# Branch gates computed in a stage of their own by Strassen's algorithm, through DRAM scratch

## The chip, the cores and the metric

The kernel runs on one core of a Trainium2 chip. The metric is the device time of one execution in microseconds; of several runs the median is taken. PE is the matrix engine, DVE the vector engine, ACT the scalar engine, POOL the GpSimd engine; SP only issues DMAs. Each engine works through its own queue in order.

## The reference

One step of a diffusion backbone with one layer, 1024 features, 1024 latent tokens and 256 context tokens. Cut to what matters here:

```python
mod = (silu(cond) @ w_ada + b_ada)[:, None, :]
sh1, sc1, gt1, sh2, sc2, gt2 = split(mod, 6)
u = rmsnorm(x, g_norm1) * (1 + sc1) + sh1
xp, su, sv, q, k, v, o_pre, gate_pre, br_pre = split(u @ w_in, points)
y_a, y_b, y_c = pool_branch(xp), sgu_branch(su, sv), mlstm_branch(q, k, v, o_pre, gate_pre)
branches = einsum('btrc,rcd->btrd', stack([y_a, y_b, y_c]), w_branch)
gates = sigmoid(br_pre).reshape(B, T, 3, 1024)
x = x + gt1 * (sum_r(gates * branches) @ w_out)
u2 = rmsnorm(x, g_norm2) * (1 + sc2) + sh2
x = x + gt2 * (relu(u2 @ w_ff1) ** 2 @ w_ff2)
```

`cond` differs between latent and context tokens, so each part of `mod` has two rows. All inputs and results are float32.

## The kernel before

Features lie on the 128 partitions and tokens along the free axis, in three groups of columns: 512 and 512 latent tokens and 256 context tokens (`GROUPS`). Every float32 product is made of three products of a reduced type: an operand is split into `hi` (a cast) and `lo` (the rest), and hi*hi, hi*lo and lo*hi are summed in PSUM. ACT makes the cast of a weight (L94) and DVE the rest (L95). A projection of 1024 features to a tile of 128 therefore takes 8 x 3 matmuls per group of columns (`dense`, L118 to L126). PSUM has eight banks: three of the tag `mm`, for projections, and five of the tag `sd`.

The stages follow one another: norms and adaLN; the mLSTM heads; the SGU's v projection; the pooling branch; the SGU branch, which for each of four tiles mixes (L707, evicted by DVE at L711), projects u (`p_su`, evicted by DVE at L719) and splits the product into hi and lo (L115, L116); the branch stage; the output projection and the second norm; FF1; FF2. A scheduler reorders instructions of neighbouring stages within each engine's queue, so stages overlap a little.

**The branch stage** (L734 to L769) goes over the SGU branch, the pooling branch and the mLSTM branch, and in each over eight feature tiles `d` and three groups: gate product (`br`, 24 matmuls), sigmoid on ACT (L754), branch product (`pb`, 12 matmuls, L756 to L761), and on DVE the product of the two (L766, or L768 and the sum at L769) into the merged sum in `z`. The SGU's result stays in SBUF; the other two are read back from DRAM (`scr_ya`, `scr_yc`). Weights are loaded as 512 KB tiles of two `raw` buffers.

**The adaLN pieces** (`mod_piece`, L424 to L448) are the part of `mod` that is needed only after the branches. After half of the units of the branch stage one piece is made: a 512 KB load of `w_ada`, four multiply-adds on DVE (L437, L439) into two accumulators. Each fourth piece ends a group: POOL reduces both accumulators over the partitions (L446), adds the bias `bt` (L444, L447) and writes the row to `scr_mod` (L448). There are eight groups.

**FF1** (`Pair`, L942 to L1018) is computed by a Strassen algorithm of Winograd's form already: two feature tiles and two halves of the latent tokens make a 2 x 2 block product of 7 products instead of 8, each of 4 x 3 matmuls on 512 columns. The left sides are the weight blocks and four sums of them (L1002, on DVE); the right sides are the quarters `B11` to `B22` of the activations and four sums of those, `T1` to `T4`, each split into hi and lo. The context tokens are multiplied in the ordinary way, 48 matmuls of 256 columns a pair. DVE and ACT add the products out of PSUM into `z`. During FF1, POOL makes sums of FF2's weights (L1048).

## Time and profile before

| | before |
|---|---|
| median of three runs | 2010.93 us (2009.26 to 2013.67) |
| profiled execution | 2009.92 us |
| its span, first to last instruction | 2008.1 us |
| mean granted clock | 0.994 |
| PE, DVE, ACT, POOL busy | 97%, 59%, 39%, 19% |
| branch stage, DVE and POOL busy from 700 to 750 us | 18.20 and 11.07 of 50 us |

A row of the timeline is a start, a duration, an engine, a line, an operation, its output and inputs, and a count; in brackets stands the idle time of the engine ahead of it and what ended it. A row of the waits names who waited for whom: total, times, longest. Rows that group instructions by line end with busy time, mean ns of one, and the idle time ahead of them. Matmuls overlap in the array, so the distance between two starts, not the duration shown, is what one of them costs. Line numbers are those of the kernel the row comes from; order rows of the kernel after the change have its own lines.

### The profile page before, as it was taken

To read this page: it belongs to the slowest core of one execution; us is meant where nothing else is said; L and a number is where in the kernel's file an instruction comes from. 1 tells how busy PE (TensorE), PEld (TensorE's weight loads), DVE (VectorE), ACT (ScalarE), POOL (GpSimd) and SP (SyncE) were. 2 spreads that over 40 slices of the span, in tenths; PEclk is the share of its full clock that TensorE was granted. 3 is DMA by queue.
4 is the path that set the end of the run, shared out by engine and by line. 5 is a ranking of instruction groups with operands and counts; after the bars stand their busy time and mean duration, and the time that the engine had idled before them with its cause. 6 is when DMAs were issued, how large, how long until landed. Compare 5 with 4: busy or idle time off the path is not lost. (4 is left out here: it accounts for less than half of the span.)

```text
span 2008.1 us, 28473 instructions
## 1 busy us (share of the span) xinstructions
PE 1948.0 (97%) x10688; PEld 1677.5 (84%) x10688; DVE 1182.4 (59%) x1997; ACT 793.0 (39%) x1620; POOL 375.3 (19%) x372
## 2 busy tenths in 40 slices
PE   6999999998999999999999998999999999999997
PEld 3788888996888888888889997888888878888886
DVE  6684443448753235445526678887776665654675
ACT  6634454653211111111114465444445545443443
POOL 2000001108211122222201004444431120000002
PEclk9999999999999999999999999999999999999999
DMA  8011111113321252244215444677774496655544
GB/s 327 22 35 48 51 45 42 60 46 102 140 65 62 64 188 75 74 130 143 84 32 200 168 135 175 245 252 250 252 274 137 155 357 218 191 177 157 155 136 154
DMA packets 122683, 282.30 MB, mean 141 GB/s; under 512 B 14256, under 2 KB 28464, under 8 KB 120496
## 3 DMA queue, kind: packets, MB, share of 16 engines
q1 hardware_dynamic: 85456, 199.12, 30.8%
q0 software_dynamic: 14240, 53.56, 7.0%
q10 hardware_dynamic: 22848, 27.80, 3.9%
q8 instruction: 84, 1.38, 0.3%
q14 instruction: 55, 0.45, 0.1%
HBM read 204.36 MB, written 76.06 MB: 140 GB/s over the span
## 5 line engine op out<-in xcount | busy, mean ns | idle before, releaser
L754 ACT ACTIVATE sg<-br 128x512 f32<-128x512 f32 (+1 forms) x72 | 37.9, 526 | 305.3 <-PE br L126 290.4
L1048 POOL TENSOR_TENSOR z<-z 128x512 f32<-128x512 f32 x64 | 96.9, 1515 | 119.6 <-DMA z<-in_w_ff 109.9
L446 POOL PARTITION_ALL_REDUCE acc<-acc x16 | 54.2, 3430 | 325.8 <-DVE acc L439 325.8
L439 DVE SCALAR_TENSOR_TENSOR acc<-wb,scond,acc 128x512 f32<-128x512 f32 x112 | 82.3, 791 | 17.1 <-DMA wb<-in_w_ada 16.9
L768 DVE TENSOR_TENSOR sg<-pb,sg 128x512 f32<-128x512 f32 (+1 forms) x48 | 28.7, 599 | 101.8 <-PE pb L761 96.8
L1153 POOL TENSOR_TENSOR rs_y<-rs_y,neghalf 128x1 f32<-128x1 f32 x10 | 9.1, 912 | 333.9 <-DVE rs_y L1152 333.8
L766 DVE TENSOR_TENSOR z<-pb,sg 128x512 f32<-128x512 f32 (+1 forms) x24 | 14.4, 600 | 79.6 <-PE pb L761 79.6
L960 ACT ACTIVATE z<-z 128x512 f32<-128x512 f32 x64 | 40.6, 634 | 47.2 <-DVE z L1011 34.9
L95 DVE TENSOR_TENSOR lo_br<-raw_br,hi_br 128x1024 fp32r<-128x1024 f32 x24 | 37.5, 1564 | 28.1 <-ACT hi_br L94 27.9
L94 ACT CAST hi_br<-raw_br 128x1024 fp32r<-128x1024 f32 x24 | 25.2, 1050 | 70.2 <-DMA raw_br<-in_w_in 40.7
L131 POOL TENSOR_TENSOR rs_h<-rs_h,neghalf 128x4 f32<-128x4 f32 (+1 forms) x12 | 11.9, 992 | 207.9 <-DVE rs_h L130 207.8
L1002 DVE TENSOR_TENSOR z<-z 128x512 f32<-128x512 f32 x64 | 45.6, 716 | 0.6
L1039 POOL DMA_DIRECT2D scr_s<-x x48 | 26.5, 552 | 92.9 <-DVE x L1033 85.2
L583 DVE SCALAR_TENSOR_TENSOR yc<-th,ccol,z 128x512 f32<-128x512 f32 (+1 forms) x12 | 7.9, 660 | 57.3 <-PE th L581 57.3
L961 ACT ACTIVATE z<-z 128x512 f32<-128x512 f32 x64 | 40.4, 631 | 1.5
L94 ACT CAST hi_wb<-raw_wb 128x1024 fp32r<-128x1024 f32 x12 | 12.6, 1047 | 63.8 <-PE br L125 44.0
L95 DVE TENSOR_TENSOR lo_wo<-raw_wo,hi_wo 128x1024 fp32r<-128x1024 f32 x24 | 29.2, 1220 | 14.1 <-ACT hi_wo L94 14.1
L865 ACT ACTIVATE po<-z 128x256 f32<-128x256 f32 x40 | 15.5, 387 | 52.4 <-DVE z L864 45.8
L666 POOL TENSOR_TENSOR z<-z 128x1024 f32<-128x1024 f32 (+13 forms) x20 | 35.4, 1781 | 3.0 <-ACT z L651 3.0
L769 DVE TENSOR_TENSOR z<-z,sg 128x512 f32<-128x512 f32 (+1 forms) x48 | 34.7, 724 | 1.2
L862 DVE TENSOR_TENSOR po<-po,gt 128x256 f32<-128x256 f32 x40 | 17.1, 428 | 26.4 <-PE po L860 23.2
L447 POOL TENSOR_TENSOR acc<-acc,bt 1x512 f32<-1x512 f32 x16 | 20.7, 1309 | 58.3 <-issue 58.3
(3368 smaller groups left out, 7293.3 us busy)
## 6 DMA issues: line engine op xcount, KB each, us to landing
z<-in_w_ff SPq DMA_DIRECT2D x64, 512.0 KB, 5.2
wb<-in_w_ada SPq DMA_DIRECT2D x32, 512.0 KB, 3.7
scr_t<-z POOLq DMA_DIRECT2D x16, 1024.0 KB, 5.2
raw_br<-in_w_in SPq DMA_DIRECT2D x24, 512.0 KB, 3.4
raw_wo<-in_w_out SPq DMA_DIRECT2D x24, 512.0 KB, 4.2
scr_h<-z ACTq DMA_DIRECT2D x48, 256.0 KB, 4.4
scr_s<-x POOLq DMA_DIRECT2D x48, 256.0 KB, 3.1
wa<-in_w_ada SPq DMA_DIRECT2D x32, 256.0 KB, 5.2
```

What stands on the lines that cost most here:

```text
L94: A.copy(hi, raw)
L95: eng.tensor_tensor(lo, raw, hi.bitcast(F32), ALU.subtract)
L439: V.scalar_tensor_tensor(acc[j], wa[:, k2, :], scond[:, k, j : j + 1], acc[j], ALU.mult, ALU.add)
L446: G.partition_all_reduce(acc[j], acc[j], P, bass.bass_isa.ReduceOp.add)
L666: eng.tensor_tensor(at(dst, a, b), at(src, a - l, b - l), at(src, a + r_, b + r_), ALU.add)
L754: A.activation(sg[:, :n], ps[:, :n], AF.Sigmoid)
L768: V.tensor_tensor(sg[:, :n], pb[:, :n], sg[:, :n], ALU.mult)
L769: V.tensor_tensor(mg(d, g), mg(d, g), sg[:, :n], ALU.add)
L960: A.activation(t, t, AF.Relu)
L961: A.activation(t, t, AF.Square)
L1002: V.tensor_tensor(out, x, y, op)
L1048: G.tensor_tensor(out, x, y, ALU.subtract)
```

## The change

1. **A gate stage.** After the SGU, the 24 gate tiles are computed as 12 pairs by the FF1 algorithm (`GatePair`, a subclass of `Pair`): 84 matmuls of 512 columns and 48 of 256 per pair. The four weight sums are on POOL (`eng` is `G`; for FF1 it stays DVE). ACT applies the sigmoid, and ACT's queue stores the gates to `scr_g`, five halves of a tile a pair of features.
2. **Right sides.** `quarter_sums` rebuilds the 16 raw quarters of `u` as hi + lo and subtracts them into the four sums, 32 DVE operations, written behind the SGU's first tile. `split_sum` splits T4, T3, T2 and T1 around the first two pairs.
3. **The branch stage** has branch products alone. All three branches, the SGU's too (`scr_yb`), and the gates are read from DRAM into slots on SP's queue.
4. **adaLN pieces** are 64 of 256 KB instead of 32 of 512 KB, all in the gate stage: after pair n, up to piece 6n. Their raws lie in `z`.
5. **Pools.** The pools of weight and temporary tiles are closed ahead of the gates. One pool (`q1`: four tiles `e`, six `th`, six `w`, where it had five, six `s`) serves gates, branches, output projection and FF1; weights are loaded in halves of 512 columns (`load_half`). `slot` has 59 buffers, where it had 60. FF2 takes every second raw tile from `s`.

The diff, cut to its core:

```diff
-    sp = pa.enter_context(tc.tile_pool(name="sp", bufs=60))
+    sp = pa.enter_context(tc.tile_pool(name="sp", bufs=59))
...
-    def mod_piece(i):
-        b, kk = i // 4, i % 4
...
+    def mod_piece(i, raw):
+        b, k = i // 8, i % 8
...
+        SP.dma_start(raw, w_ada[k * P : (k + 1) * P, 2048 + b * 512 : 2048 + (b + 1) * 512])
+        for j in range(2):
+            if k == 0:
+                V.tensor_scalar(acc[j], raw, scond[:, k, j : j + 1], None, ALU.mult)
+            else:
+                V.scalar_tensor_tensor(acc[j], raw, scond[:, k, j : j + 1], acc[j], ALU.mult, ALU.add)
+        if k < 7:
             return
...
+    def quarter_sums(raw):
+        for kk in range(4):
+            b11, b21, b12, b22 = raw["B11"][kk], raw["B21"][kk], raw["B12"][kk], raw["B22"][kk]
+            if raw is u_raw:
+                for t, k, g in ((b11, kk, 0), (b12, kk, 1), (b22, kk + 4, 1), (b21, kk + 4, 0)):
+                    hi, lo = uT[k][g]
+                    V.tensor_tensor(t, hi.bitcast(F32), lo.bitcast(F32), ALU.add)
+            for out, x, y in ((b11, b12, b11), (b12, b22, b12), (b22, b22, b11), (b21, b22, b21)):
+                V.tensor_tensor(out, x, y, ALU.subtract)
...
         proj(I_SU + ci, f"su{ci}", ev_su)
-        ys.append(parts)
+        if ci == 0:
+            quarter_sums(u_raw)
...
+                self.eng.tensor_tensor(out, x, y, op)
+            ps = self.prod(self.w22, "T4")
+            A.copy(self.b2, ps)
+            ps = self.prod(split(a11, f"s2_{self.name}"), "T2")
...
+    for n in range(NGP):
+        if n not in gates:
+            gate_pair(n)
+            gates[n].begin()
+            gates[n].contexts()
+        gates[n].rest()
+        gates[n].store(ORDER[n // 4], n % 4 * 2)
+        del gates[n]
+        while n > 0 and piece < 64 and piece < 6 * n:
+            mod_piece(piece, zs(12 + piece % 4))
+            piece += 1
...
-            w = load_w(w_in[I_BR + r * KT + d], f"br{r}_{d}")
...
-                ps = ps_mm(f"br{r}_{d}_{g}")
-                dense(ps, w, uT, g)
-                sg = tmp(f"sg{r}_{d}_{g}")
-                A.activation(sg[:, :n], ps[:, :n], AF.Sigmoid)
+                sg = slot(f"sg{r}_{d}_{g}", F32)
+                SP.dma_start(sg[:, :n], scr_g[r][d][:, t0 : t0 + n])
```

The order of instructions on DVE in the SGU stage. Before, between the last evictions of the pooling branch (`ya`) and those of the first SGU tile (`mt`, with `p_su` its projection in PSUM):

```order
566 L690 SCALAR_TENSOR_TENSOR ya_0_1_4909<-pp_0_4906,ccol,ya_0_0_4908 128x512
567 L690 SCALAR_TENSOR_TENSOR ya_1_1_4918<-pp_1_4915,ccol,ya_1_0_4917 128x512
568 L690 SCALAR_TENSOR_TENSOR ya_2_1_4927<-pp_2_4924,ccol,ya_2_0_4926 128x256
569 L711 SCALAR_TENSOR_TENSOR mt_0_4939<-mx_0_4934,ccol,z 128x512
570 L711 SCALAR_TENSOR_TENSOR mt_1_4946<-mx_1_4941,ccol,z 128x512
571 L719 TENSOR_TENSOR mt_0_4939<-mt_0_4939,p_su_4959 128x512
```

After, the same place on DVE, where L704 and L706 are the quarter sums and L686, L737 and L744 stand for L690, L711 and L719:

```order
589 L704 TENSOR_TENSOR z<-u2h_421,u2l_422 128x512
590 L686 SCALAR_TENSOR_TENSOR ya_1_1_4919<-pp_1_4916,ccol,ya_1_0_4918 128x512
591 L706 TENSOR_TENSOR z<-z 128x512
592 L686 SCALAR_TENSOR_TENSOR ya_2_1_4928<-pp_2_4925,ccol,ya_2_0_4927 128x256
593 L706 TENSOR_TENSOR z<-z 128x512 x2
594 L737 SCALAR_TENSOR_TENSOR mt_0_4940<-mx_0_4935,ccol,z 128x512
595 L737 SCALAR_TENSOR_TENSOR mt_1_4947<-mx_1_4942,ccol,z 128x512
596 L706 TENSOR_TENSOR z<-z 128x512
597 L737 SCALAR_TENSOR_TENSOR mt_2_4952<-mx_2_4949,ccol,z 128x256
598 L737 SCALAR_TENSOR_TENSOR mt_0_5092<-mx_0_5087,ccol,z 128x512
599 L706 TENSOR_TENSOR z<-z 128x512
600 L744 TENSOR_TENSOR mt_0_4940<-mt_0_4940,p_su_4960 128x512
```

Up to DVE's row 552 both orders agree; from there to row 600 the order after has 28 of the 32 new operations ahead of the first multiplication by `p_su`.

The order on POOL, where an all-reduce is an `ISA` row with its accumulator, and an `ISA` row without one stands ahead of a change to another kind of instruction. Before, in the branch stage, one group of adaLN pieces:

```order
102 L446 ISA
103 L446 ISA acc_0_5442<-acc_0_5442 128x512
104 L446 ISA acc_1_5443<-acc_1_5443 128x512
105 L444 DMA bt_5597<-in_b_ada 1x16x32
106 L447 ISA
107 L447 TENSOR_TENSOR acc_0_5442<-acc_0_5442,bt_5597 1x512
108 L447 TENSOR_TENSOR acc_1_5443<-acc_1_5443,bt_5597 1x512
109 L448 DMA scr_mod<-acc_0_5442 16x1x32
110 L448 DMA scr_mod<-acc_1_5443 16x1x32
```

After, in the gate stage, the second group's all-reduce and the sums of gate pair 3 (L848), with the next group's all-reduce behind them:

```order
114 L442 ISA acc_0_6181<-acc_0_6181 128x512
115 L442 ISA acc_1_6182<-acc_1_6182 128x512
116 L848 ISA
117 L848 TENSOR_TENSOR z<-z 128x512 x3
118 L440 DMA bt_6408<-in_b_ada 1x16x32
119 L848 TENSOR_TENSOR z<-z 128x512
120 L443 TENSOR_TENSOR acc_0_6181<-acc_0_6181,bt_6408 1x512
121 L443 TENSOR_TENSOR acc_1_6182<-acc_1_6182,bt_6408 1x512
122 L444 DMA scr_mod<-acc_0_6181 16x1x32
123 L444 DMA scr_mod<-acc_1_6182 16x1x32
124 L442 ISA
125 L442 ISA acc_0_6416<-acc_0_6416 128x512
```

Weight sums, on which PE's product T2 depends, now stand in one queue with the all-reduces, in turns.

## The prediction

> **What bounds the kernel now.** I read the page first, then busy time in windows over the stages that change, then PE's waits there, then the timeline of PE, DVE and POOL where work is added.

> The page, share of each engine; below it stretches of 50 us (PE, weight loads, DVE, ACT, POOL; granted clock, DMA share, GB/s), and what PE waited for from 450 to 1200 us:

> ```profile
> PE 1948.0 (97%) x10688; PEld 1677.5 (84%) x10688; DVE 1182.4 (59%) x1997; ACT 793.0 (39%) x1620; POOL 375.3 (19%) x372
> ```
> ```profile
> 500.00:550.00 50.00, 47.76 (x248) 39.19 (x249) 37.46 (x52) 12.87 (x19) 12.82 (x17) 0.93 0.37 130
> 550.00:600.00 50.00, 50.00 (x272) 43.44 (x270) 25.78 (x43) 5.89 (x7) 2.83 (x1) 1.00 0.23 70
> 700.00:750.00 50.00, 50.00 (x263) 43.12 (x262) 18.20 (x24) 8.14 (x12) 11.07 (x7) 1.00 0.60 190
> ...
> 1200.00:1250.00 50.00, 44.66 (x239) 36.59 (x238) 44.70 (x79) 31.90 (x66) 19.17 (x12) 1.00 0.44 160
> 1300.00:1350.00 50.00, 50.00 (x268) 43.25 (x266) 39.54 (x54) 23.66 (x44) 22.98 (x24) 1.00 0.74 258
> ```
> ```profile
> PE pp L686 <- DVE xp L684: 5.4, 1, 5.4
> PE pp L686 <- issue: 3.1, 1, 3.1
> PE fB L938 <- ACT a_0h L929: 1.2, 1, 1.2
> PE po L860 <- DVE lo_wo L95: 0.5, 1, 0.5
> ```

> The branch stage (549 to 1042 us) is pure PE: 50.00 of 50 us, full clock, no wait of PE after 502 us, DVE at a third. Fewer matmuls there are time won one for one, as long as the new stage feeds PE as well. FF1 (1300 us), the model of the new gate stage, also reaches 50.00, with DVE at 39.5 of 50 and POOL at 23.

> **Part 1, matmuls removed.** One of the profile's modelled matmul durations (0.39) is no price; the distance between starts is. Twelve steps of 512 columns (517.34 to 520.06) and 23 of 256 (526.76 to 529.50):

> ```profile
> 517.34 0.39 PE L126 MATMUL p_su<-u0h,lo_su 128*128 128x512 f32 x1
> 520.06 0.39 PE L126 MATMUL p_su<-u4h,lo_su 128*128 128x512 f32 x1
> ...
> 526.76 0.28 PE L124 MATMUL p_su<-u0c,hi_su 128*128 128x256 f32 x1
> 529.50 0.28 PE L126 MATMUL p_su<-u7c,lo_su 128*128 128x256 f32 x1
> ```

> That is 0.227 and 0.119 us each. Before, two gate tiles cost 96 + 48 matmuls, 27.5 us; after, 84 + 48, 24.8 us. Twelve pairs save 144 x 0.227 = **32.7 us**. The branch products keep their count (24 tiles x (24 x 0.227 + 12 x 0.119) = 165 us).

> **Part 2, quarter sums in the SGU stage.** DVE gets 16 additions hi + lo (L704) and 16 subtractions (L706) of 128x512, in its queue ahead of the evictions that PE waits for. The order keeps DVE's rows up to the end of this L673, at 507.4:

> ```profile
> 505.77 1.63 DVE L673 TENSOR_TENSOR z<-z 128x1024 f32<-128x1024 f32 x1
> 507.43 1.10 DVE L684 TENSOR_TENSOR xp<-z,xp 128x512 f32<-128x512 f32 x1
> 508.46 0.74 DVE L690 SCALAR_TENSOR_TENSOR ya<-pp,ccol,ya 128x512 fp32r<-128x512 f32 x1
> 509.12 1.72 DVE L684 TENSOR_TENSOR xp<-z,xp 128x512 f32<-128x512 f32 x1
> ...
> 512.01 1.23 DVE L666 TENSOR_TENSOR z<-z 128x1024 f32<-128x1024 f32 x1
> 513.15 1.22 DVE L95 TENSOR_TENSOR lo_su<-raw_su,hi_su 128x1024 fp32r<-128x1024 f32 x1
> 514.29 1.63 DVE L673 TENSOR_TENSOR z<-z 128x1024 f32<-128x1024 f32 x1
> 515.84 0.74 DVE L690 SCALAR_TENSOR_TENSOR ya<-pp,ccol,ya 128x512 fp32r<-128x512 f32 x1
> ...
> 526.60 0.68 DVE L719 TENSOR_TENSOR mt<-mt,p_su 128x512 f32<-128x512 f32 x1
> ```
> ```profile
> 529.62 2.40 PE L707 MATMUL mx<-z,vn 128*128 128x128 f32 x20
> 531.77 0.47 PE L124 MATMUL p_su<-u0h,hi_su 128*128 128x512 f32 x1
> ```

> A 512-column operation of two SBUF inputs costs 0.61 (half of 1.22). Rows are priced from start to next start where one follows another (L690 0.66, 0.4 at 256 columns; L666 1.14; L673 1.55), L684 at 1.10. From 507.4 to the multiplication (L744) that reads p_su_4960 out of PSUM stand 28 new operations (17.1), four L684 (4.4), nine L690 (5.2), L666 and L673 (2.7), two L95 (2.4) and four L711 (2.4), 34.2 in all; it ends at 507.4 + 34.2 + 0.6 = 542.2. PE comes a tile's ten mx matmuls (2.15 from start to start, each on two rows of the trace) later than before to its next projection, at 531.8 + 2.15 = 533.9, and means to start p_su_5112, for which that bank must be free. PE stands **8.3 us**. Ends: 4 (some sums find gaps, such as the 5.4 us in which PE waited before) and 12 (each sum at 0.74 or beside POOL). Afterwards DVE's chain per tile is shorter than PE's.

> **Part 3, the start of the gates.** The first weight casts on ACT stand behind yb3's stores to DRAM, and 16 splits of the sums are written between those of the first pairs. Before, FF1 began the same way: 1.2 us on a_0h, and 5.3 us of PE idle from 1200 to 1250, with DVE at 44.70 (rows above). I take **+3.7** (2 to 8).

> **Part 4, POOL in the gates.** Everything else is decided here. Every gate pair's four weight sums (L848) run on POOL; FF1's ran on DVE (L1002). And the adaLN pieces, formerly spread over the whole branch stage, now come within 12 pairs, their all-reduces in the same POOL queue, in order: all-reduce 2, sums of pair 3; 3, pair 4; 4, pair 6; 5, pair 7; 6, pair 8; 7, pair 10; 8, pair 11. POOL's prices, from the page and one all-reduce's timeline:

> ```profile
> L1048 POOL TENSOR_TENSOR z<-z 128x512 f32<-128x512 f32 x64 | 96.9, 1515 | 119.6 <-DMA z<-in_w_ff 109.9
> L446 POOL PARTITION_ALL_REDUCE acc<-acc x16 | 54.2, 3430 | 325.8 <-DVE acc L439 325.8
> L447 POOL TENSOR_TENSOR acc<-acc,bt 1x512 f32<-1x512 f32 x16 | 20.7, 1309 | 58.3 <-issue 58.3
> ```
> ```profile
> 597.17 6.78 POOL L446 PARTITION_ALL_REDUCE acc<-acc  x2 [79.40 <-DVE acc L439]
> 603.84 0.71 POOL L444 DMA_DIRECT2D bt<-in_b_ada  x1
> 612.03 2.52 POOL L447 TENSOR_TENSOR acc<-acc,bt 1x512 f32<-1x512 f32 x2 [7.49 <-issue]
> 614.51 1.21 POOL L448 DMA_DIRECT2D scr_mod<-acc  x2
> ```

> Between an all-reduce and the next ordinary addition POOL stands 58.3 / 8 = 7.3 us each time, waiting for nothing that shows. The gap belongs to the kind of instruction changing; I call it a switch. Before, nobody waited for it. After, sums stand behind each all-reduce, so it lies between PE and its weights. Whether the way back, from additions to an all-reduce, costs the same can't be seen: each all-reduce came after tens of us of idleness (79.40 here) that would hide it. Its bounds are 0 and the largest such gap, some 7.5; I take 7.2, since it is the same kind of change.

> [...]

> POOL's loop in consecutive all-reduce pairs: switch 7.3, three sums 4.5, bt 0.7, fourth sum 1.5, two L447 2.5, two L448 1.2, switch 7.2, two all-reduces 6.8 = **31.7 us, against 24.8 of PE**. Were the second switch free, DVE closes a loop of its own: the first s split waits for the third sum; behind it on DVE stand up to 11 accumulations, three splits and an addition, and the next all-reduce waits for the last accumulation. From this row four take 2.73:

> ```profile
> 705.47 2.73 DVE L439 SCALAR_TENSOR_TENSOR acc<-wb,scond,acc 128x512 f32<-128x512 f32 x4
> 649.49 2.48 DVE L439 SCALAR_TENSOR_TENSOR acc<-wb,scond,acc 128x512 f32<-128x512 f32 x1
> ```

> 11 x 0.683 + 4 x 0.61 = 10, with some contention 11; then 6.8 + 7.3 + 4.5: 29.6 in all. So a pair whose all-reduce comes hard upon another's loses 31.7 - 24.8 = 6.9 us on its T2 product, which needs the third sum, or 4.8 with the second switch free. Those are pairs 4, 7, 8 and 11. Pairs 2 and 3 hide it, since POOL makes the sums of pairs 0 and 1 early. Pairs 6 and 10 come after a pair without an all-reduce, in which POOL needs 6.1 of 24.8 us and makes up its arrears; I leave them 1 each. 4 x 6.9 + 2 = **29.6 us** (20 with the second switch free). Were POOL never late, I would leave 2 to 6.

> DVE itself has 8 splits, 7 additions and 16 accumulations per pair, 20 us of 24.8: near, not over. But one accumulation took 2.48 rather than 0.68 beside an all-reduce (second row).

> [...]

> By rows of FF1, a split took 0.69 alone and 1.21 and 1.51 beside POOL's sums:

> ```profile
> 1302.47 0.69 DVE L930 TENSOR_TENSOR s_3l<-z,s_3h 128x512 fp32r<-128x512 f32 x1 [1.34 <-PE fT L939]
> ...
> 1312.52 1.21 DVE L930 TENSOR_TENSOR a_4l<-z,a_4h 128x512 fp32r<-128x512 f32 x1 [2.66 <-PE fB L939]
> ...
> 1315.62 1.51 DVE L930 TENSOR_TENSOR a_5l<-z,a_5h 128x512 fp32r<-128x512 f32 x1 [0.19 <-ACT a_5h L929]
> ```

> Two operations beside each pair of all-reduces, 1.8 longer, and four beside sums, 0.8 longer, make 7 us; 27 in place of 20. That is a rival below.

> **Part 5, gates to branches.** The y loads (10 half tiles, two parts, 5.2 MB) take slots that the last pair's matmuls hold until about 20 us before its end. At 258 GB/s (1300 row) they take 20 us. **+2** (0 to 6). In the branch stage proper, DMA's some 32 MB (gates 15.7, y 10.5, weights 6.3) over 165 us are 195 GB/s, and DVE has some 3.4 of 6.9 us: 0.

> **Part 6, later pools.** The `w` ring with six tiles, half loads, and FF2's raws in two pools touch stages that waited 1.2 and 0.5 us as above. **-1** (-4 to +4).

> **Sum.** -32.7 + 8.3 + 3.7 + 29.6 + 2 - 1 = **+9.9** on the profiled execution's 2009.92 us, so 2019.8; the median of the runs shown, 2010.93, lies 1.0 above that execution: **2021 us**.

> **The rivals.**
> (a) The saving stands: POOL isn't late, because the second switch is free and the accumulations finish early. Part 4 becomes 4, and the median 2010.9 - 32.7 + 8.3 + 3.7 + 4 + 2 - 1 = 1995. For it: FF1's POOL was busy 23 of 50 without loss. Against: the 7.3 gap ahead of the sums, which is known. It decides once both loops are under 24.8: both switches together under 7.6, and DVE's chain behind the first s split under 6.2, which is so if most accumulations run ahead of that split.
> (b) The second switch is free and DVE's loop holds: part 4 is 20, and the median 2010.9 - 32.7 + 8.3 + 3.7 + 20 + 2 - 1 = 2011, no change. For it: no row shows that switch. Against: a change of kind cost 7.3 in the other direction, eight times of eight.
> (c) The DVE queue decides too: the 27 us of DVE per pair with an all-reduce adds about 2 us for each of eight to a loop that goes over DVE, and part 2 reaches 12: 2021 + 8 to 16, 2033. For it: the 2.48. Against: DVE at 39.5 of 50 in FF1 beside POOL at 23, without loss.

> **How the numbers follow.** Forecast 0.45, (a) 0.25, (b) 0.18, (c) 0.12. Below about 4 us (0.2%) runs of this kernel can't be told from no change; they spread by 4.4. The range leaves out the outer half of (a) and of (c): 1994 to 2033. Faster 0.30 (a, and the lower 0.05 of b), same 0.13 (the rest of b), slower 0.57.

> **What the profile after would show.** Right: PE waits on p_su about 8 us near 534; on T2 of pairs 4, 7, 8 and 11 (L772 to L774 behind s splits), 5 to 8 us each, with POOL's sums late; POOL gaps ahead of both all-reduce and sums; the gates lasting 298 + 33 us. Wrong: no PE wait on s splits in pairs 7 and 8 (then (a)); gaps before sums alone (then (b)); PE waiting on accumulations' neighbours in pairs without an all-reduce, 5 and 9 (then (c)); PE standing at the y loads or in branch products on sg, which I hold at 2.

## The result, and the profile after

The changed kernel takes 2082.1 us (median of four runs, 2081.6 to 2084.7), the kernel before 2011.6 in the same session: a ratio of 1.035, 95% interval 1.0335 to 1.0371. The profiled execution has a span of 2080.5, before 2008.1: **72.4 us longer, where 9.9 were forecast**; the range ended at 2033 us, 22 above the kernel before.

Stages go by the first matmul of each (first gate product, first branch product, first of the output projection, of FF1, of FF2). Both kernels' and the experiments' lengths in us, from the profiles. Of the experiments e7 was run four times and the others once, and stages that no edit touches begin up to 5 us apart (gates start at 588.7 in e1 and 593.9 in e8), so lengths of stages say more here than totals:

| kernel | gates start | gates | branches | output projection | FF1 | FF2 | span |
|---|---|---|---|---|---|---|---|
| before | - | - | ends 1073.6 | 123.2 | 417.1 | 394.2 | 2008.1 |
| after | 588.9 | 349.7 | 165.6, ends 1104.2 | 123.1 | 415.0 | **438.2** | 2080.5 |
| e1, FF2 raws in a ring of their own | 588.7 | 350.0 | 165.6 | 122.6 | 415.1 | **396.7** | 2038.7 |
| e2, quarter sums on POOL | **579.4** | 348.3 | 165.6 | 123.2 | 415.3 | 434.8 | 2066.6 |
| e3, adaLN pieces in the branch stage | 593.4 | **304.5** | 319.2 with the next | | 414.7 | 432.6 | 2064.4 |
| e4, gates' sums on DVE | 588.8 | **312.2** | 167.2 | 123.8 | 415.4 | 432.6 | 2040.0 |
| e5, no additions on POOL | 589.8 | 338.6 | 167.3 | 121.7 | 415.4 | 435.5 | 2068.3 |
| e6, matmuls in the gates' waits | 590.6 | 357.5 | 165.5 | 122.0 | 415.5 | 434.5 | 2085.6 |
| e7, three edits together | 580.7 | 310.5 | 166.7 | 122.0 | 415.1 | 398.8 | **1993.8** |
| e8, matmuls in FF2's waits | 593.9 | 350.3 | 165.6 | 121.7 | 415.1 | 434.8 | 2081.4 |

So the 72 us came at two places: 30.6 up to the output projection (10.9 forecast), and 44.0 in FF2 (next to none). The page after, and its 50-us windows (PE, weight loads, DVE, ACT, POOL; granted clock, DMA share, GB/s):

```profile
PE 1948.5 (94%) x10544; PEld 1670.3 (80%) x10544; DVE 1328.8 (64%) x2237; ACT 853.6 (41%) x1780; POOL 444.3 (21%) x420
```
```profile
500.00:550.00 50.00, 41.98 (x199) 32.50 (x200) 49.80 (x72) 12.03 (x18) 13.53 (x16) 0.90 0.38 137
...
800.00:850.00 50.00, 40.49 (x180) 32.78 (x181) 31.62 (x35) 12.78 (x24) 27.65 (x22) 0.86 0.33 108
...
950.00:1000.00 50.00, 50.00 (x264) 43.09 (x264) 19.01 (x32) 4.97 (x8) 0.00 (x0) 1.00 0.90 312
...
1750.00:1800.00 50.00, 40.83 (x170) 33.27 (x169) 37.95 (x66) 25.77 (x50) 0.00 (x0) 0.90 0.70 214
1800.00:1850.00 50.00, 50.00 (x222) 41.41 (x221) 23.99 (x38) 19.79 (x33) 0.00 (x0) 1.00 0.59 187
```

PE's busy time is what it was (1948.0): 144 matmuls fewer, but others at half speed, their starts 0.43 apart in place of 0.227. Where PE stands (800, 1750), the granted clock is below 1 as well, 0.86 and 0.90. The waits of PE, largest first:

```profile
PE w L1274 <- ACT r_1h L1174: 34.1, 3, 15.8
...
PE pp L682 <- DVE xp L680: 7.2, 2, 3.8
PE fT_g L791 <- ACT s_g7h L773: 6.5, 1, 6.5
PE fT_g L791 <- ACT s_g11h L773: 5.5, 1, 5.5
...
PE fT_g L791 <- ACT s_g4h L773: 3.4, 1, 3.4
```

The first row is new. FF2 makes seven products one after another, and after three of them PE waits for the cast of the next product's second right-hand tile, r_1. At the first such place, on PE, SP, DVE and ACT:

```profile
1759.30 0.39 PE L1276 MATMUL w<-r_0l,l_0h 128*128 128x512 f32 x1
1768.86 0.80 PE L1274 MATMUL w<-r_1h,l_1h 128*128 128x512 f32 x1 [9.18 <-ACT r_1h L1174]
1769.45 0.63 PE L1275 MATMUL w<-r_1h,l_1l 128*128 128x512 f32 x1
1769.88 0.63 PE L1274 MATMUL w<-r_1h,l_1h 128*128 128x512 f32 x1
1770.31 0.63 PE L1275 MATMUL w<-r_1h,l_1l 128*128 128x512 f32 x1
```
```profile
1761.14 0.32 SPq L1196 DMA_DIRECT2D l_10r<-scr_s  x1
1761.74 0.32 SPq L1185 DMA_DIRECT2D r_1r<-scr_t  x1
```
```profile
1758.14 0.68 DVE L1241 TENSOR_TENSOR c<-accU,w 128x512 f32<-128x512 f32 x1
...
1761.03 0.68 DVE L1214 TENSOR_TENSOR z<-z,c 128x512 f32<-128x512 f32 x1
```
```profile
1767.58 0.63 ACT L1219 ACTIVATE junk_y<-z 128x512 f32<-128x512 f32 x1 [2.19 <-issue]
...
1768.21 0.60 ACT L1174 CAST r_1h<-r_1r 128x512 fp32r<-128x512 f32 x1
```

The tile for r_1 comes from the pool `s`, and so do the evictions' `c` and `junk_y`, six tiles in turn. r_1 takes the turn of the third eviction's `c`, given up at 1761.03 + 0.68 = 1761.7, and there its load is issued; the cast then stands on ACT behind the last `junk_y`. This load is issued 7 us ahead of its use. Before, the tile had a ring of its own, and its load ran far ahead; in e1 below, where it has one again, the load is issued at 1722.9 and used at 1757.8.

In the gates the mechanism is close to the one forecast. POOL from one pair's all-reduce to the next, pairs 7 and 8, then the last accumulations on DVE ahead of the first of these all-reduces, and the page's row of all of them:

```profile
786.57 6.49 POOL L442 PARTITION_ALL_REDUCE acc<-acc  x2 [7.36 <-DMA z<-in_w_in]
800.19 3.93 POOL L848 TENSOR_TENSOR z<-z 128x512 f32<-128x512 f32 x3 [7.14 <-issue]
804.07 0.71 POOL L440 DMA_DIRECT2D bt<-in_b_ada  x1
804.81 1.29 POOL L848 TENSOR_TENSOR z<-z 128x512 f32<-128x512 f32 x1
806.56 2.94 POOL L443 TENSOR_TENSOR acc<-acc,bt 1x512 f32<-1x512 f32 x2 [0.47 <-DMA bt<-in_b_ada]
809.46 1.00 POOL L444 DMA_DIRECT2D scr_mod<-acc  x2
818.56 3.25 POOL L442 PARTITION_ALL_REDUCE acc<-acc  x1 [8.10 <-DVE acc L436]
```
```profile
782.24 2.07 DVE L436 SCALAR_TENSOR_TENSOR acc<-z,scond,acc 128x512 f32<-128x512 f32 x3
```
```profile
L442 POOL PARTITION_ALL_REDUCE acc<-acc x16 | 54.8, 3468 | 83.6 <-DVE acc L436 55.1
```

From 786.57 to 818.56 are 32.0 us, where 31.7 were forecast; the gap ahead of the sums is 7.1, that ahead of the all-reduce 7.4 and 8.1. The second switch shows in the first of these rows: at 786.57 POOL stood 7.4 us although DVE's last accumulation had ended 2.3 us before (784.3), and the load that the row names is of weights, which the all-reduce does not read. The 8.1 is not a switch alone, as it ended with an accumulation on DVE, and so did 55.1 of the 83.6 us that POOL stood ahead of all-reduces. With a switch of 7.4 behind the stores, which end at 810.5, POOL would have been ready at 817.9 (an estimate). So DVE's chain closed this round, 0.7 us behind POOL's: the two loops are about equally long. PE at the same place, where T2 starts with the first s split:

```profile
804.83 0.80 PE L791 MATMUL fT_g<-t2h,s_g7h 128*128 128x512 f32 x1 [6.52 <-ACT s_g7h L773]
...
807.73 0.63 PE L792 MATMUL fT_g<-t2l,s_g7h 128*128 128x512 f32 x1
808.16 0.63 PE L793 MATMUL fT_g<-t2h,s_g7l 128*128 128x512 f32 x1
808.59 0.63 PE L791 MATMUL fT_g<-t2h,s_g7h 128*128 128x512 f32 x1
```

Not forecast are the starts 0.43 apart behind the wait, where 0.227 is full speed.

### The profile page after: what moved, and what is told of

Its sections match the earlier page's. It is cut to its first block, busy times and chain, and to the rows that moved or that the text cites. A ratio compares the mean times of both kernels' runs of the same rounds, so it can differ in the third digit from the quotient of the medians.

```text
span 2080.5 us, 29153 instructions
## 1 busy us (share of the span) xinstructions
PE 1948.5 (94%) x10544; PEld 1670.3 (80%) x10544; DVE 1328.8 (64%) x2237; ACT 853.6 (41%) x1780; POOL 444.3 (21%) x420
## 5 line engine op out<-in xcount | busy, mean ns | idle before, releaser
L1115 POOL TENSOR_TENSOR z<-z 128x512 f32<-128x512 f32 x64 | 98.6, 1541 | 120.0 <-DMA z<-in_w_ff 117.4
L848 POOL TENSOR_TENSOR z<-z 128x512 f32<-128x512 f32 x48 | 64.5, 1345 | 158.2 <-DVE a_g0l L774 80.4
L436 DVE SCALAR_TENSOR_TENSOR acc<-z,scond,acc 128x512 f32<-128x512 f32 x112 | 88.6, 839 | 0.0
L442 POOL PARTITION_ALL_REDUCE acc<-acc x16 | 54.8, 3468 | 83.6 <-DVE acc L436 55.1
L1081 ACT ACTIVATE z<-z 128x512 f32<-128x512 f32 x64 | 40.5, 632 | 60.7 <-DVE z L857 28.1
L873 ACT ACTIVATE z<-z 128x512 f32<-128x512 f32 x48 | 30.3, 632 | 65.4 <-DVE z L857 35.2
L848 DVE TENSOR_TENSOR z<-z 128x512 f32<-128x512 f32 x64 | 54.6, 855 | 1.4
L782 ACT CAST hi_wb<-raw_wb 128x512 fp32r<-128x512 f32 x24 | 14.7, 621 | 99.0 <-PE pb L953 79.7
L1274 PE MATMUL w<-r_1h,l_1h 128*128 128x512 f32 x28 | 14.3, 509 | 34.1 <-ACT r_1h L1174 34.1
L970 POOL DMA_DIRECT2D z<-in_xs x10 | 5.3, 535 | 175.7 <-DVE m1l L967 132.0
L1082 ACT ACTIVATE z<-z 128x512 f32<-128x512 f32 x64 | 40.3, 629 | 1.1
L782 ACT CAST hi_wo<-raw_wo 128x512 fp32r<-128x512 f32 x48 | 28.6, 617 | 21.2 <-PE po L1049 14.7
L783 DVE TENSOR_TENSOR lo_wo<-raw_wo,hi_wo 128x512 fp32r<-128x512 f32 x48 | 32.5, 687 | 6.8 <-ACT hi_wo L782 6.6
L1274 PEld LDWEIGHTS w<-r_1h,l_1h 128*128 128x128 f32 x28 | 6.8, 244 | 36.9 <-ACT r_1h L1174 35.4
L1052 DVE TENSOR_TENSOR po<-po,gt 128x256 f32<-128x256 f32 x40 | 17.0, 431 | 28.7 <-PE po L1050 26.4
```

What stands on the lines that cost most here:

```text
L436: V.scalar_tensor_tensor(acc[j], raw, scond[:, k, j : j + 1], acc[j], ALU.mult, ALU.add)
L442: G.partition_all_reduce(acc[j], acc[j], P, bass.bass_isa.ReduceOp.add)
L782: A.copy(hi, raw)
L783: V.tensor_tensor(lo, raw, hi.bitcast(F32), ALU.subtract)
L848: self.eng.tensor_tensor(out, x, y, op)
L873: A.activation(t, t, AF.Sigmoid)
```

## The experiments

**e1: FF2's raw tiles.** Theory: turns shared with the evictions. Rival: too few tiles.

```diff
-        elif fp % 2:
-            raw = tmp2(f"r{i}_{fp}r")
```

> FF2's right-hand raw tiles come from a ring of their own with two buffers; none comes from the pool that the evictions use. Theory (shared rotation: the first odd raw tile of a product waits until the evictions of the product before have given up their temporary tiles): FF2 falls from 438 us to 394 to 400, the three waits of PE on r_1h go, 2038 to 2044 us in all. Rival (too few raw tiles: before there were four of their own): with only two in all, FF2 stays at 438 or grows, 2080 to 2100.

2040.7 us; FF2 took 396.7. With only two tiles, half as many as before the change, but none shared, the waits on r_1h are gone; PE's waits in FF2 are now these:

```profile
PE w L1272 <- ACT c_0h L1174: 2.4, 2, 2.2
PE w L1272 <- DVE z L864: 0.8, 1, 0.8
```

The shared turn was the cause, not the number of tiles: 41.5 us.

**e2: the quarter sums.**

```diff
-            quarter_sums(u_raw)
+            quarter_sums(u_raw, Pinned(tc, G))
```

> The 32 quarter sums of u move from DVE to POOL, behind POOL's last work of the pooling branch. Theory (they delay DVE's evictions by the 8.3 us of the prediction): the second SGU tile's projection starts near 534 rather than 542.6, and the total falls by 8 to 10, to 2072 to 2074. Rival (some 45 us on POOL make T4 late): PE waits for T4 in gate pair 0, and the total is 2080 or more.

2068.4. The gates start at 579.4 in place of 588.9, 9.5 us earlier (0.6 of it from stages ahead of these), and take 348.3: T4 was not late. The forecast's 8.3 is borne out; the changed kernel's trace also has the end of DVE's queue to 0.4 us, with 542.2 forecast. But PE's waits are not the one forecast, 8 us on p_su near 534. They come earlier and in pieces, as the sums also delay evictions of the pooling branch (xp, ya):

```profile
528.36 3.83 PE L682 MATMUL pp<-xp,z 128*128 128x512 f32 x6 [3.39 <-DVE xp L680]
...
536.24 2.15 PE L733 MATMUL mx<-z,vn 128*128 128x128 f32 x16 [1.15 <-DVE ya L686]
539.09 3.26 PE L733 MATMUL mx<-z,vn 128*128 128x128 f32 x24 [0.70 <-DVE mt L737]
542.60 0.50 PE L124 MATMUL p_su<-u0h,hi_su 128*128 128x512 f32 x1 [0.25 <-DVE mt L744]
```

Of the 13.7 us between the totals another 3.4 are FF2's, which varies with a wait on c_0h between kernels with the same FF2.

**e3: the adaLN pieces in the branch stage**, the bias added on DVE ahead of the all-reduce.

```diff
-        while n > 0 and piece < 64 and piece < 6 * n:
-            mod_piece(piece, zs(12 + piece % 4))
-            piece += 1
...
+                if piece < 64:
+                    mod_piece(piece, slot(f"wm{piece}", F32))
+                    piece += 1
```

> The adaLN pieces move out of the gate stage into the branch stage, one piece per unit, and the bias is added on DVE ahead of the all-reduce, so that POOL changes kind once only. Theory (all-reduces and two switches of POOL between the weight sums of successive pairs): the gate stage falls from 350 us to 304 to 312, no wait of PE on s splits from pair 3 on, the branch stage grows by 0 to 10; 2038 to 2050 in all. [...]

2066.3, so the total missed its range (4.5 us of it stand ahead of the gates). The gates did what the theory said, 304.5 us, with POOL's sums still beside DVE's splits. But DVE had no room in the branch stage, and the cost moved to the output projection: the two together take 319.2, 30.5 more than in the changed kernel. DVE's window there (third pair of numbers), and PE's waits from 898 to 1220 us:

```profile
1000.00:1050.00 50.00, 45.91 (x238) 38.68 (x237) 50.00 (x80) 5.19 (x9) 17.46 (x12) 1.00 0.78 273
```
```profile
PE po L1049 <- ACT po L1056: 18.1, 2, 17.5
PE po L1050 <- DVE m6l L968: 5.7, 1, 5.7
```

**e4: the gates' weight sums on DVE**, pieces and all-reduces where they are.

```diff
-            [uT[k][2] for k in range(KT)], G)
+            [uT[k][2] for k in range(KT)], V)
```

> The gates' weight sums move from POOL to DVE, as in FF1; pieces and all-reduces stay where they are. Theory (POOL's loop): the sums no longer stand behind an all-reduce, DVE takes 2.7 us more of a pair, some 23 of 24.8; the gate stage falls from 350 to 310 to 325, 2042 to 2057 in all. Rival (DVE is what binds): the gate stage stays at 345 or grows.

2041.8. The gates take 312.2, 37.5 less, and DVE bears it: in these 50 us it is full, and PE hardly waits.

```profile
750.00:800.00 50.00, 49.76 (x263) 42.63 (x263) 49.24 (x67) 17.46 (x32) 18.77 (x14) 1.00 0.54 170
```

**e5: POOL's loop shortened**, the two additions off POOL.

```diff
+        for j in range(2):
+            V.tensor_tensor(acc[j][0:1, :], acc[j][0:1, :], bt, ALU.add)
...
-            G.tensor_tensor(acc[j][0:1, :], acc[j][0:1, :], bt, ALU.add)
```

> The bias is added to the accumulators on DVE ahead of the all-reduce; POOL's two additions behind the sums go, and nothing else. Theory (POOL's loop of 31.7 us is what PE waits for): without 2.5 to 3.0 us of additions the loop is 28.7 to 29.2, the waits in pairs 4, 7, 8 and 11 shrink by 2.5 to 3 each, the half-speed stretches behind them too; the gate stage falls from 350 to 328 to 340. Rival (DVE's 11 accumulations close a loop of 29.6 of their own, or DVE's load binds): it falls by less than 8, as DVE has 10 us more to do.

2070.0. Gates 338.6, of which 4.4 are a new wait of the first branch product for its weights; to the last gate product 334.2. It falls by 11 to 15, inside the theory's band and more than the rival's 8. But the waits did not all shrink by the same: pairs 7 and 8 keep 3.9 and 3.0, pair 11 has none, and pair 9 has a new one of 4.8. Five of the eight all-reduces now start within 0.4 us of DVE's last work on their accumulators, so DVE's chain is no shorter there than POOL's.

**e6: PE kept busy in the gates' waits**, 24 idle matmuls ahead of T2 in pairs 4, 7, 8 and 11, to see whether the half speed goes with PE's idle time.

```diff
+                            Pinned(tc, PE).matmul(
+                                idle, self.w22[0][:, k * P : k * P + P], self.right_["T4", k][x % 2],
...
             ps = self.prod(split(a11, f"s2_{self.name}"), "T2")
```

> In gate pairs 4, 7, 8 and 11, ahead of the product T2, PE makes 24 matmuls on ready operands into a spare bank that nobody reads, 5.5 us each time, 21.8 in all. [...]

2087.6; the gates took 357.5, 7.8 longer. The clock did rise, to 0.90 in the window that had 0.86 above:

```profile
800.00:850.00 50.00, 39.49 (x178) 32.38 (x177) 27.64 (x29) 11.78 (x22) 27.85 (x22) 0.90 0.28 88
```

But the kernel was no clean test: the fillers pushed aside context products of the next pair that stood in these waits before (eleven ahead of pair 7's), and these were then missing later. Inconclusive by its time.

**e7: three edits together**, those of e1 (with three tiles), e2 and e4.

> Three edits on the changed kernel together: FF2's raw tiles from a ring of their own with three buffers, the quarter sums on POOL, the gates' weight sums on DVE. Theory (the three costs are separate and add): 2082 - 42 - 11 - 40 = 1989 us, 0.989 of the kernel before, the Strassen saving of 32.7 less some 12 of waits. Rival (mending one lets another wait grow, DVE's load in the gates above all): 2000 to 2015.

1994.6 us, 0.989 of the kernel before (interval 0.9876 to 0.9909): **faster than both**, and than the kernel before by 1.1%. It is 5.6 above the sum of the parts. The gates took 310.5 and FF2 398.8, the latter with a wait of 4.0 on c_0h. The same windows as above:

```profile
800.00:850.00 50.00, 49.87 (x264) 42.80 (x263) 38.75 (x58) 19.06 (x35) 13.38 (x9) 1.00 0.43 138
...
1750.00:1800.00 50.00, 50.00 (x223) 41.39 (x222) 25.23 (x40) 19.91 (x34) 0.00 (x0) 1.00 0.56 164
```

**e8: the clock, cleanly.** The fillers add a tile of zeros to sums that PE is about to extend, where it only waits.

```diff
+            if fp == 0 and i in (6, 5, 3):
+                for _ in range(38):
+                    PE.matmul(banks[0], nil, rt[0][0], start=False, stop=False)
```

> The changed kernel, with 38 matmuls by a tile of zeros (8.6 us) behind the first right-hand tile of the three FF2 products that wait for r_1h; they add nothing to the sums and stand where PE waits in any case, 9.3, 9.3 and 15.9 us. Theory (a wait of PE brings the half-speed clock behind it): after the first two waits, now 0.7 us, no half-speed matmuls (11 and 11 before, 4.6 us of loss); after the third, 7.3 us, they stay; FF2 falls from 438.2 to 433 to 435. Rival (the half speed has another cause, the burst of DMA or of DVE work there): the half-speed matmuls stay, and FF2 is 437 to 440.

2083.3; FF2 434.8, in the theory's band, though e2 with an unchanged FF2 reads the same and the time alone decides nothing. The clock decides: windows around the first two waits and the third, with the fillers, then in the changed kernel without:

```profile
1760.00:1800.00 40.00, 39.42 (x174) 32.32 (x173) 30.73 (x55) 20.37 (x42) 0.00 (x0) 1.00 0.73 223
1930.00:1970.00 40.00, 39.42 (x175) 32.29 (x173) 31.34 (x55) 19.82 (x39) 0.00 (x0) 1.00 0.59 186
2000.00:2040.00 40.00, 32.87 (x137) 26.74 (x136) 31.08 (x55) 20.52 (x40) 9.96 (x15) 0.91 0.67 224
```
```profile
1760.00:1800.00 40.00, 31.14 (x127) 25.57 (x128) 30.34 (x52) 22.85 (x44) 0.00 (x0) 0.87 0.81 247
1930.00:1970.00 40.00, 30.82 (x128) 25.01 (x127) 29.18 (x51) 19.00 (x38) 0.00 (x0) 0.87 0.60 188
2000.00:2040.00 40.00, 24.25 (x101) 19.67 (x100) 32.83 (x58) 21.86 (x43) 9.95 (x15) 0.79 0.67 224
```

DMA and DVE work about as much as before in them. Where the wait is filled to 0.6 us, the clock stays at 1.00, in place of 0.87; where 7.1 us are left, it is 0.91. At these places the half speed goes with PE's own idle time.

## Why the prediction was wrong

The direction was right, and so in the main was the mechanism that it rested on, POOL's loop in the gates; but two thirds of the 62 us that are missing come from FF2, which it priced at next to nothing. Step by step:

- **Part 1, matmuls**: -32.7. Right: the branch stage after takes 165.6 (165 forecast), and e3's gates, without POOL's trouble, 304.5: 298, a wait of 2.8 and the slow matmuls behind two waits at the start. (The branch stage lies from 578 to 1074 us, not from 549 to 1042; its length is right.)
- **Part 2, quarter sums**: +8.3, measured +9.5 (e2). The size and the end of DVE's queue are right, the wait is not: PE stood 0.2 us on p_su, and 5.6 on xp, ya and mt ahead of it.
- **Parts 3 and 4, gates**: 33.3 of waits. The waits of PE between 588 and 940 us add up to 34.7: 5.3 at the start (3.7), 6.5 and 0.7 in pair 7 (6.9), 5.5 and 0.7 in pair 11 (6.9), 4.6 in pair 4 (6.9), 3.8 in pair 8 (6.9), 2.8 and 3.0 in pairs 6 and 10 (1 each), 1.6 in pair 3 and 0.2 in pair 9 (none). The single pairs are off by up to 3, and that the sum is not is partly luck. **But the stage lasted 51.7 longer than the 298 of its matmuls**, although 2.5 of these waits lie ahead of its first one. By the distances between starts, steps with a wait in them cost 35 more than at full speed, and some 90 other matmuls, at about half speed, lose 16. This second term wasn't in the sum, although the kernel before shows it: 0.93 in the window from 500 to 550, behind its wait of 5.4.
- **Part 4, the second switch**: taken at 7.2 between bounds of 0 and 7.5, measured 7.4 where DVE's accumulations were done. Rival (a) falls, and of rival (b) the free switch; that DVE's chain closes the loop came out true beside it, as shown above, at 32.0 in place of 29.6. Of rival (c), DVE's load: one half is true, since with the sums on DVE it is full (e4), but it still fed PE. The forecast counted 16 accumulations per pair; six pieces of two make 12, so its 20 and 27 us of DVE per pair are too high. Rival (b)'s part 4, 4 x 4.8 + 2, is 21.2 and not 20.
- The traces show a gap in both directions: 7.1 ahead of additions at 800.19, 7.4 ahead of an all-reduce at 786.57, and 6.0 ahead of one in e5 at 834.86, where the profile names a split on DVE as what ended it and no accumulation.
- **Part 5, y loads**: +2, measured 0; the first branch product starts 0.2 us behind the last gate product.
- **Part 6, later pools**: -1, between -4 and +4; measured -2.1 in FF1 and **+44.0 in FF2**. This is the step that failed. The prediction priced the edit of FF2's raws by two waits of other stages, 1.2 and 0.5 us; its rows of PE's waits end at 1200 us, ahead of FF2. It named the two pools, and didn't ask in whose turn the next tile comes. 37.5 us are waits (34.1 and 3.2 and 0.2), the rest half speed.

With the two terms put right, the half speed's 16 in the gates and part 6 at 44.0 - 2.1 = 41.9 in place of -1, the forecast would have been 9.9 + 16 + 42.9 = 68.8, against 72.4.

## What to carry to other kernels

When a tile moves into a pool with other users, write out the turns: a load that should run ahead waits for the tile that had the buffer one round earlier, and if that is an eviction's, the prefetch ends at the eviction. Price a wait of PE with the slow matmuls behind it, 1.7 to 2.4 us for each of FF2's three long waits here. When an engine makes two kinds of instruction in turns and stands between them, as POOL did for 6.0 to 7.9 us, have the kind that others wait for made elsewhere: e4 moved four short operations a pair and won 37 us.

## What the runs showed of the hardware

```profile
684.85:688.26 3.41, 1.84 (x9) 1.12 (x8) 2.48 (x2) 2.52 (x5) 3.02 (x4) 1.00 0.32 116
688.26:691.67 3.41, 3.41 (x9) 2.64 (x8) 3.41 (x4) 0.14 (x1) 3.15 (x4) 0.50 0.42 120
691.67:695.08 3.41, 3.41 (x20) 2.98 (x19) 3.41 (x6) 0.48 (x1) 0.00 (x0) 1.00 0.38 103
```

In pair 6 waits of 1.1 and 1.7 us, which end at 771.95 and 777.92, left it at 1.00. At one place in FF2, on c_0h, a wait of 0.8 us (before) was followed by no slow matmul, one of 3.2 (after) by eight. How long PE must stand for the clock to fall, no run here was made to show.

A product with zeros kept the clock up as other work did: e8's fillers multiply by a tile of zeros, and it stayed at 1.00 in the two windows that read 0.87 without them.
